# Stick-breaking attention without the "less one" step, with more of the FFN in the hand-made order

## The chip, the cores and the metric

One Trainium2 chip, of which the kernel uses one core. The metric is device time of one execution, in microseconds (us). Engines are named as the profile names them: PE (TensorE matmul), PEld (TensorE weight load), DVE (VectorE), ACT (ScalarE), POOL (GpSimd), SP (SyncE, which here mostly issues DMAs).

## The reference, cut to what matters

One decoder layer on x of 1024 tokens x 1024 features, float32:

```
h = rms_norm(x);  q, k, v, glu_a, glu_b = split(h @ w_in)      # 512 columns each
q, k normed per head of 64
beta[t,s] = sigmoid(q_t . k_s / 8),  s < t
A[t,s]    = beta[t,s] * prod_{s<j<t} (1 - beta[t,j])
attn_t    = sum_{s<t} A[t,s] v_s                               # 8 heads
c = swish(layer_norm(causal_conv31(glu_a * sigmoid(glu_b))))
x = x + concat(attn, c) @ w_out
h = rms_norm(x);  gate, val = split(h @ w_up)                  # 2816 columns each
x = x + (silu(causal_conv3(gate)) * val) @ w_down
```

With S[t,s] the product of (1 - beta[t,j]) over s <= j < t, and S = 1 from s = t on, a weight is the difference A[t,s] = S[t,s+1] - S[t,s]. So the sum over s can be made with S itself and the differences of neighbouring v, plus the last v of the range. The kernel before uses S - 1 in place of S, for which that last v drops out.

## The kernel before, in words

All products that need float32 accuracy are made of three matmuls in the fast type fp32r (`mm3`, L389 to L391): high times high, high times low, low times high. So each operand is first cast to its high part, on ACT mostly, and the low part is the difference, on DVE mostly. A matmul here has 128 x 128 weights and 512 columns; transposes are matmuls of 128 columns.

The kernel has three stretches. Two of them are laid out by a planner (`Plan`): every step is added with an engine or a choice of engines with a price in ns for each, with what it comes after and which buffers it takes, and `plan.run(ORDERS[0])` or `ORDERS[1]` walks through a written-out list of step numbers, picks the cheaper engine for the steps with a choice, and so fixes what stands in each engine's queue and in which order. Each engine then works through its queue in order and waits at the first instruction that isn't ready.

1. First plan. Idle matmuls at the start (`begin`, L485; five more at L499 that wait for the first input, L494). x is squared (ACT L530), its root taken (POOL L533, L534), scaled (DVE L548), transposed on PE to `hT` (L556) and split into `h_hi` (ACT L560) and `h_lo` (DVE L561). The weights of v are scaled by the norm's gain into `hi_v` (ACT L593) and `lo_v` (DVE L599); L715 makes v. v is differenced (POOL L656). q, k and the two glu halves follow, the convolution on DVE, ACT and POOL, then the attention. A head has four groups of 256 queries. For each row block of 128 queries PE makes z (L1304, L1305), ACT makes sigmoid(-z) into one of four buffers `nb` (L1312), DVE turns it into the running product from the right (the scan, L1326), POOL, or ACT, subtracts one in place ("less", L1331, L1333), PE transposes it, 128 x 128 at a time, into `wT` (L1353), which is split into a high part (ACT L1362, L1364, sometimes DVE) and a low part (DVE L1369, L1374) and multiplied with the differenced v into the bank `po` (L1381). The blocks on the diagonal have a half that isn't written; it is cleared to zero once. Two groups, one of each half of `po`, end in a copy (ACT L1409) and a sum (DVE L1412) into `attn`. Between these, PE does the convolution's half of w_out as filler (`op`); its weights are split by ACT L1438 and DVE L1439, those of the attention's half (`hio`, `loo`) by ACT L1526 and DVE L1531.
2. Second plan. The attention's half of w_out (`opa`; its operand `m` is split by ACT L1599, L1607 and DVE or POOL L1605, L1608), the second norm (DVE L1622, L1640, ACT L1632), transposes to `h2T` (PE L1648) and their split (`b`, `bT`: ACT L1660, DVE or POOL L1661; copies and sums of them at L1673, L1693 to L1698). FFN up works on quarters of its operands with seven products in place of eight, named 11, 12, 22, S1 to S4 after the sums that go in; sums of the weights are made at L1733 to L1739 and L1795, their splits at L385, L386, L1784 and L1788. The first two products of the first column block (f = 0) lie in this plan.
3. The rest, without a planner: FFN up for the remaining products of 22 column blocks, its gate (L1834, L1836), and FFN down (`dn`, L1987).

DMAs are issued on SP in the order in which the plan puts them.

## Time and profile before

| | us |
|---|---|
| median of 3 runs (lowest to highest) | 1103.04 (1102.15 to 1103.22) |
| the profiled execution | 1100.73 |
| its span in the trace | 1099.0 |
| PE busy | 1085.8 |
| DVE, ACT, POOL busy | 875.4, 606.6, 609.8 |
| granted TensorE clock | 1.00 in all stretches |

Lines of a timeline read: start, duration, engine, line of the code, operation, out<-in, shape, xcount of equal neighbours, and in brackets how long the engine (or the instruction) waited before it and on whom. Lines of the table by stretch read: from:to, length, then busy time and count of PE, PEld, DVE, ACT, POOL, the granted clock, the share of the DMA engines and GB/s. A busy PE overlaps with the next instruction, so a matmul that lasts 0.39 us in a timeline starts about 0.23 us behind the one before it. Lines of the grouped views give a count, the busy time and the mean in ns, or min/median/max in ns.

### The profile page before, as it was taken

What the parts mean: (1) busy time and instruction counts of PE and PEld (TensorE: products, weight loads), DVE (VectorE), ACT (ScalarE), POOL (GpSimd) and SP (SyncE); (2) the same over time, 40 slices, a digit from 0 to 9 for tenths busy, and PEclk for the clock granted to TensorE, in tenths of its full rate; (3) what the DMA queues carried; (4) which work ended last, traced back from release to release, by engine and by line L of the source; (5) the groups of instructions that cost most, each with busy time, mean ns of one, the idle gap of its engine ahead of it and who ended that gap; (6) DMA issues with size and microseconds to landing.
All of it is one profiled execution on the core that took longest, in us unless ns stands there. A gap on an engine that the chain in (4) does not pass through costs nothing.

```text
span 1099.0 us, 14945 instructions
## 1 busy us (share of the span) xinstructions
PE 1085.8 (99%) x5252; PEld 904.1 (82%) x5252; DVE 875.4 (80%) x1178; ACT 606.6 (55%) x1113; POOL 609.8 (55%) x540
## 2 busy tenths in 40 slices
PE   8999999999999999999999999999999999999998
PEld 5888888889888878778888888888888888888887
DVE  6498898689998996899977777677867578697885
ACT  7345467878877665644433333333433388676660
POOL 3377988786654544784333223313322399887760
PEclk9999999999999999999999999999999999999999
DMA  8121210444643324523322312222222572413403
GB/s 272 39 58 52 83 39 19 116 154 143 203 125 97 106 94 161 187 58 116 96 96 67 104 59 96 77 96 77 77 97 67 183 287 78 153 31 124 153 7 147
DMA packets 110249, 117.99 MB, mean 107 GB/s; under 512 B 21114, under 2 KB 89953, under 8 KB 110175
## 3 DMA queue, kind: packets, MB, share of 16 engines
q1 hardware_dynamic: 110158, 117.05, 32.5%
q8 instruction: 41, 0.67, 0.3%
q14 instruction: 34, 0.27, 0.1%
q10 hardware_dynamic: 16, 0.00, 0.0%
HBM read 82.43 MB, written 28.31 MB: 101 GB/s over the span
## 4 chain that ended last, share of the span: by engine, by line
PE 92%; DVE 3%; ACT 1%; DMA 1%; issue 1%; POOL 1%; SPq 0%; DVEq 0%; ACTq 0%
PE dn L1987 19%; PE u_S L391 7%; PE u_S L390 7%; PE u_S L389 7%; PE u L391 5%; PE u L390 5%; PE u L389 5%; PE po L1381 3%; PE qk L389 3%; PE qk L391 3%; PE qk L390 3%; PE wT L1353 2%; PE z L1304 1%; PE glu_b L390 1%; PE op L389 1%; PE glu_b L391 1%
## 5 line engine op out<-in xcount | busy, mean ns | idle before, releaser
L1987 PE MATMUL dn<-wd,wd 128*128 128x512 f32 x768 | 181.4, 389 | 0.0
L1987 PEld LDWEIGHTS dn<-wd,wd 128*128 128x128 f32 x768 | 144.1, 188 | 29.9
L1990 DVE TENSOR_TENSOR c<-dn,c 128x512 f32<-128x512 f32 x120 | 81.4, 685 | 27.6 <-PE dn L1987 27.0
L391 PE MATMUL u_S<-bT,aS 128*128 128x512 f32 x264 | 102.7, 389 | 0.1
L390 PE MATMUL u_S<-bT,aS 128*128 128x512 f32 x264 | 102.5, 389 | 0.0
L389 PE MATMUL u_S<-bT,aS 128*128 128x512 f32 x264 | 102.5, 389 | 0.0
L385 ACT CAST aS<-rawu 128x512 fp32r<-128x512 f32 x63 | 39.0, 621 | 95.2 <-PE u_S L391 68.9
L1892 ACT CAST wd<-rawd 128x512 fp32r<-128x512 f32 x128 | 72.6, 618 | 31.8 <-DMA rawd<-act_d 8.0
L1326 DVE TENSOR_TENSOR_SCAN nb<-nb,one 128x128 f32<-128x128 f32 (+7 forms) x64 | 85.1, 1341 | 1.5 <-ACT nb L1312 1.4
L1733 POOL TENSOR_TENSOR s<-rawu 128x512 f32<-128x512 f32 x21 | 29.6, 1414 | 101.8 <-DMA rawu<-in_w_up_dram 101.8
L1891 ACT COPY whole<-rawd 128x512 f32<-128x512 f32 x110 | 63.4, 585 | 26.0 <-DVE wd L1893 12.9
L1739 POOL TENSOR_TENSOR rawu<-rawu 128x512 f32<-128x512 f32 x21 | 29.5, 1408 | 81.1 <-DVE a L386 81.1
L1893 DVE TENSOR_TENSOR wd<-whole,wd 128x512 fp32r<-128x512 f32 x90 | 59.9, 684 | 12.6 <-ACT wd L1892 6.8
L1331 POOL TENSOR_SCALAR nb<-nb 128x512 f32<-128x512 f32 (+7 forms) x57 | 39.8, 705 | 50.3 <-DVE nb L1326 38.0
L1836 DVE SCALAR_TENSOR_TENSOR y<-gv,cols_a,y 128x1023 f32<-128x1023 f32 (+1 forms) x44 | 59.9, 1361 | 8.9 <-ACT y L1834 8.9
L385 ACT CAST a<-rawu 128x512 fp32r<-128x512 f32 x63 | 38.9, 621 | 48.7 <-PE u_S L391 33.8
L389 PE MATMUL u<-b,a 128*128 128x512 f32 x168 | 65.5, 390 | 0.0
L391 PE MATMUL u<-b,a 128*128 128x512 f32 x168 | 65.4, 389 | 0.0
L390 PE MATMUL u<-b,a 128*128 128x512 f32 x168 | 65.3, 389 | 0.0
L386 DVE TENSOR_TENSOR a<-rawu,a 128x512 fp32r<-128x512 f32 x63 | 50.9, 809 | 13.3 <-ACT a L385 13.3
L1735 POOL TENSOR_TENSOR rawu<-s,rawu 128x512 f32<-128x512 f32 x21 | 32.0, 1527 | 48.6 <-DVE a L386 47.8
L391 PEld LDWEIGHTS u_S<-bT,aS 128*128 128x128 f32 x264 | 49.5, 188 | 10.7 <-DVE aS L386 0.5
(359 smaller groups left out, 3274.5 us busy)
## 6 DMA issues: line engine op xcount, KB each, us to landing
rawu<-in_w_up_dram SPq DMA_DIRECT2D x44, 512.0 KB
act_d<-y SPq DMA_DIRECT2D x22, 512.0 KB
rawd<-act_d SPq DMA_DIRECT2D x22, 512.0 KB
rawd<-in_w_down_dram SPq DMA_DIRECT2D x22, 512.0 KB
raw_qk<-in_w_in_dram SPq DMA_DIRECT2D x16, 256.0 KB
rawo<-in_w_out_dram SPq DMA_DIRECT2D x8, 512.0 KB
m<-conv_d SPq DMA_DIRECT2D x16, 256.0 KB
xt<-in_x_dram SPq DMA_DIRECT2D x8, 512.0 KB
```

The source lines that it names most:

```text
L385: nc.scalar.copy(hi, src)
L386: lo_engine.tensor_tensor(lo, src, f32(hi), op=ALU.subtract)
L389: nc.tensor.matmul(ps, a_hi, b_hi, start=first, stop=False)
L390: nc.tensor.matmul(ps, a_hi, b_lo, start=False, stop=False)
L391: nc.tensor.matmul(ps, a_lo, b_hi, start=False, stop=last)
L1326: nc.vector.tensor_tensor_scan(rev, rev, ones_of[0][:, :w], 0.0, op0=ALU.mult, op1=ALU.max)
L1836: nc.vector.scalar_tensor_tensor(y[:, j:], g[:, :S - j], par("fw", (KF - 1 - j) * NF + f), y[:, j:], op0=ALU.mult, op1=ALU.add)
L1891: nc.scalar.copy(whole, src)
L1892: nc.scalar.copy(t[:, 0], src)
L1893: lo_engine.tensor_tensor(t[:, 1], whole, f32(t[:, 0]), op=ALU.subtract)
L1987: nc.tensor.matmul(ps, a[:, tok], b, start=first and m == 0, stop=last and m == 2, skip_group_check=True)
L1990: nc.vector.tensor_tensor(sums[c][s], ps, sums[c][s], op=ALU.add)
```

## The change

The diff's parts, then its core:

- The scanned products go to the transposes as they are. The 64 "less" steps are gone. Unwritten halves of the diagonal blocks hold ones in the high part instead of zeros. For each group of 256 keys the last v joins the sum: `take_ends` issues four tiny DMAs for each half of the heads (8 in all), PE transposes them (4 transposes), DVE copies them to `v_ends`; the differencing of v waits for these DMAs as well. `summed` becomes two instructions of 256 columns that add `po`, the last v and the copy.
- 9 idle matmuls at the start instead of 7.
- More steps have a choice of engines: scaling x (ACT too), the casts to `h_hi` (DVE too), the high part of v's weights (DVE too), scaling q and k (POOL and ACT too), the low parts of both halves of w_out (POOL too). Prices in the planner are changed, some by much (the load time of DMAs from 3250 to 3500 ns).
- The second plan knows of the end of the first (two empty steps), and it also holds the remaining five products of f = 0 with their sums, and the first two products of f = 1 with their weights' load and split.
- Both lists of step numbers are new. In counts: DVE's instructions go from 1180 to 1203, ACT's from 1099 to 1030, POOL's from 545 to 506, SP's from 304 to 312, PE's from 5267 to 5275.

```diff
 ORDERS = ...
-1 35 37 14 36 49 2 0 39 41 50 38 40 45 42 3 5 8 51 43 6 16 46 55 11 44 52 119 53 122 56 130 128 15 4 121 28 125 54 25
+1 35 14 37 49 0 36 39 50 38 40 2 41 45 42 43 3 44 46 119 122 5 8 6 51 47 52 48 16 124 26 55 53 54 121 56 7 9 57 128
...
-        for n in range(7):
+        for n in range(9):
...
-            c = add("DVE", 690, lambda i=i, cols=cols: nc.vector.tensor_scalar(xt[:, cols], xt[:, cols], d["rs"], None, op0=ALU.mult),
+            c = add({"DVE": 560, "ACT": 650}, lambda eng, i=i, cols=cols: (
...
-            f = add("ACT", 600, lambda i=i, where=where: nc.scalar.copy(h_hi[t // 4][where], d["pt", i]), T(at_ + 1), [m])
+            f = add({"ACT": 600, "DVE": 690}, lambda eng, i=i, where=where: (nc.scalar.copy if eng == "ACT" else nc.vector.tensor_copy)(
+                h_hi[t // 4][where], d["pt", i]), T(at_ + 1), [m])
...
-            a = add("ACT", 1190, high, T(at_ - LEAD_W), [x, begun_at], d["rooms"])
-            b = add({"DVE2": 1400, "POOL": 3700}, low, T(at_ - LEAD_W + 0.5), [a])
+            a = add({"ACT": 1330, "DVE": 1120}, high, T(at_ - LEAD_W), [x, begun_at], d["rooms"])
+            b = add({"DVE2": 1480, "POOL": 3700}, low, T(at_ - LEAD_W + 0.5), [a])
...
+        def take_ends():
+            d["ends"] = squares(room, f"ends{blk}")[:4, :256]
+            for n in range(4):
+                nc.sync.dma_start(d["ends"][n:n + 1, :], qkv["v", blk][P - 1:P, 2 * n + 1, :])
+
+        def turn_ends():
+            d["turned"] = bank(s, [P, 2, 4], f"ends{blk}")
+            for c in range(2):
+                nc.tensor.transpose(d["turned"][:, c, :], d["ends"][:, c * P:(c + 1) * P], ident[:4, :4])
+
+        y = add("SP", 2000, take_ends, key, after, [room])
...
-            subs.append(add({"POOL": 2414}, sub, key, [x]))
+            subs.append(add({"POOL": 2414}, sub, key, [x, y]))
...
-                nc.scalar.copy(diagonal(blk, name)[:, :P], zero_b)
+                nc.scalar.activation(diagonal(blk, name)[:, :P], zero_b, AF.Identity, bias=plus_one if name == "thd" else 0.0)
...
-                def less(eng, d=d, o=o):
-                    nb = d["nb"][:, o:S]
-                    if eng == "POOL":
-                        nc.gpsimd.tensor_scalar(nb, nb, 1.0, -1.0, op0=ALU.mult, op1=ALU.add)
-                    else:
-                        nc.scalar.activation(nb, nb, AF.Identity, bias=minus_one)
-
                 a = add("DVE", 130 + 2.1 * w, scan, i - AHEAD_SCAN + 0.3 * u, ones)
-                b = add({"POOL": 192 + 0.84 * w, "ACT": 296 + 0.84 * w}, less, i - AHEAD_SCAN + 0.3 * u, [a])
-                ws.append((b, d, nbt, o))
+                ws.append((a, d, nbt, o))
...
-                def summed(dst=dst, pd=pd, pa=pa):
-                    nc.vector.tensor_tensor(dst(), pd["po"].rearrange("p a t -> p (a t)")[pa, :], dst(), op=ALU.add)
+                def summed(dst=dst, pd=pd, pa=pa, h=h, half=half):
+                    for a in range(2):
+                        to = dst()[:, a * 256:(a + 1) * 256]
+                        end = 4 * (h // 2) + 2 * half + a
+                        nc.vector.scalar_tensor_tensor(to, pd["po"][pa, a, :], v_ends[pa, end:end + 1], to, op0=ALU.add, op1=ALU.add)
...
-        b = add("DVE2", 1215, lambda: nc.vector.tensor_tensor(w_attn[k][1], d["raw"], f32(w_attn[k][0]), op=ALU.subtract), key, [a])
+        b = add({"DVE2": 1215, "POOL": 2450}, lambda eng: (nc.vector if eng == "DVE" else nc.gpsimd).tensor_tensor(w_attn[k][1], d["raw"], f32(w_attn[k][0]), op=ALU.subtract), key, [a])
...
+    attention_ends = add("PE", 2000, lambda: None, -9.0)
+    last_sums = add("DVE", 790, lambda: None, -8.0, [add("ACT", 690, lambda: None, -8.5, [attention_ends])])
...
-        for e, a, b in ((e11, "11", "11"), (e12, "12", "21")):
-            add("PE", 2730, lambda a=a, b=b: begun.update({a: product_up(0, A, a, b)}), BEGIN_AT, e + block_done[b], [plan.token("o")])
+        _, x1, x2 = first_two(0, ready, BEGIN_AT, [])
+        key = BEGIN_AT + 1
...
+        first_two(1, next_ready, key, attn_read)
+        q, tq = product(0, "S4", "22", key + 0.2, e_s4)
+        s2p, t2 = product(0, "S2", "T2", key + 0.4, e_s2)
...
+        s3p, t3 = product(0, "S3", "T3", key + 0.7, e_s3)
...
+        s1p, t1 = product(0, "S1", "T1", key + 1.0, e_s1)
...
+        p22, t22 = product(0, "22", "T4", key + 1.3, e22)
```

What the new lists do to the engines' queues is shown at three places. The first is PE's queue at the start, from the first transposes of h on; before:

```order
L556 MATMUL hT_0_223<-ident_r,x_k_138 128x128 x4
L556 MATMUL hT_1_245<-ident_r,x_k_138 128x128 x4
L556 MATMUL hT_0_255<-ident_r,x_k_138 128x128 x4
L715 MATMUL v_260<-hi_v_228,h_hi_175 128x512 x2
L556 MATMUL hT_1_266<-ident_r,x_k_138 128x128 x4
L715 MATMUL v_260<-hi_v_240,h_lo_176 128x512
```

and in the changed kernel:

```order
L556 MATMUL hT_0_225<-ident_r,x_k_138 128x128 x4
L556 MATMUL hT_1_236<-ident_r,x_k_138 128x128 x4
L739 MATMUL v_241<-hi_v_231,h_hi_175 128x512 x2
L556 MATMUL hT_0_258<-ident_r,x_k_138 128x128 x4
L739 MATMUL v_241<-hi_v_231,h_lo_176 128x512 x2
L556 MATMUL hT_1_271<-ident_r,x_k_138 128x128 x4
```

The first two products of v now stand ahead of the transposes of the second row of tiles of x. With them, ACT casts the first `h_hi` ahead of everything else and scales the second tile of x, and DVE scales the first two pieces of v's weights.

The second place is DVE's queue at the end of the attention (head 7, its last group): the scan of the last row block, casts and low parts of wT, low parts of w_out (`loo`), the sum; before:

```order
L1531 TENSOR_TENSOR loo2_4296<-rawo_3078,hio2_4295 128x1024
L1326 SCALAR_TENSOR_TENSOR nb0_7_2432<-nb0_7_2432,one_2173 128x1024
L1374 TENSOR_TENSOR tl_2354<-wT7_2_0_4319,rest_2182 128x512
L1364 CAST rest_2182<-wT7_2_1_4331 128x512
L1374 TENSOR_TENSOR tl_2354<-wT7_2_1_4331,rest_2182 128x512
L1369 TENSOR_TENSOR diagonal_1_3285<-wT7_2_2_4337,diagonal_1_3285 128x384
L1374 TENSOR_TENSOR tl_2354<-wT7_3_0_4359,rest_2182 128x512
L1531 TENSOR_TENSOR loo1_4348<-rawo_3078,hio1_4347 128x1024
L1369 TENSOR_TENSOR diagonal_1_3285<-wT7_3_3_4364,diagonal_1_3285 128x384
L1374 TENSOR_TENSOR tl_2354<-wT7_3_1_4382,rest_2182 128x512
L1374 TENSOR_TENSOR tl_2354<-wT7_3_2_4391,rest_2182 128x512
L1531 TENSOR_TENSOR loo3_4404<-rawo_3078,hio3_4403 128x1024
```

and in the changed kernel:

```order
L1355 SCALAR_TENSOR_TENSOR nb0_2_2246<-nb0_2_2246,one_2085 128x1024
L1395 TENSOR_TENSOR tl_2352<-wT7_2_0_4257,rest_2156 128x512
L1390 TENSOR_TENSOR diagonal_1_3336<-wT7_2_2_4266,diagonal_1_3336 128x384
L1395 TENSOR_TENSOR tl_2352<-wT7_2_1_4273,rest_2156 128x512
L1395 TENSOR_TENSOR tl_2352<-wT7_3_0_4279,rest_2156 128x512
L1385 CAST rest_2156<-wT7_3_1_4299 128x512
L1395 TENSOR_TENSOR tl_2352<-wT7_3_1_4299,rest_2156 128x512
L1390 TENSOR_TENSOR diagonal_1_3336<-wT7_3_3_4305,diagonal_1_3336 128x384
L1395 TENSOR_TENSOR tl_2352<-wT7_3_2_4321,rest_2156 128x512
L1556 TENSOR_TENSOR loo3_4345<-rawo_3323,hio3_4344 128x1024
L1436 SCALAR_TENSOR_TENSOR attn_110<-po7_2_4256,v_ends_103,attn_110 64x256 x2
```

Two low parts of w_out have left DVE here; they stand in POOL's queue, as does a third one earlier. Behind the sum the casts of `m` on ACT stand in the same order as before.

The third place is PE's queue in the second plan where FFN up begins; before, from the last opa product of token tile 7 on:

```order
L391 MATMUL opa7_1_4909<-hio2_4295,m7_4800 128x512
L1648 MATMUL h2T3_0_4931<-ident_r_118,h2_3_4899 128x128 x4
L1648 MATMUL h2T3_1_4938<-ident_r_118,h2_3_4899 128x128 x4
L389 MATMUL u0_11_4957<-b11_4435,a_first_4893 128x512
L390 MATMUL u0_11_4957<-b11_4435,a_first_4893 128x512
```

and in the changed kernel:

```order
L390 MATMUL opa7_1_4825<-hio2_4214,m7_4737 128x512
L1678 MATMUL h2T3_0_4849<-ident_r_118,h2_3_4804 128x128 x4
L1678 MATMUL h2T3_1_4855<-ident_r_118,h2_3_4804 128x128 x4
L1678 MATMUL h2T6_1_4861<-ident_r_118,h2_6_4734 128x128 x4
L388 MATMUL u0_11_4889<-b11_4368,a_first_4819 128x512
L389 MATMUL u0_11_4889<-b11_4368,a_first_4819 128x512
```

Four transposes of token tile 6 now stand between those of tile 3 and the first product. Behind u0_11 and u0_12 come the transposes of tile 7, then u1_12 and u1_11 (before: u1_11, u1_12), and then S3, S2, S1, 22, S4 of f = 0 (before: S2, S3, S1, S4, 22). On POOL this stretch now also holds more of the sums and low parts of the weights of f = 1.

More of the change, by code (lines that the diff above doesn't have):

```diff
@@ L651, in differences @@
         x.moves = [Plan.FEW, Plan.MIXED, Plan.FEW] * 2
+        room, s = plan.token("squares"), plan.token("s")
+        def take_ends():
[7 more added lines that the diff above has]
+        y = add("SP", 2000, take_ends, key, after, [room])
+        y.moves = [Plan.FEW] * 4
+        m = add("PE", 230, turn_ends, key, [y], [s])
+        kept_ends = add("DVE", 100, lambda: nc.vector.tensor_copy(v_ends[:, 8 * blk:8 * blk + 8].rearrange("p (c t) -> p c t", c=2), d["turned"]), key, [m])
+        room.users += [y, m]
+        s.users += [kept_ends]
+        done["ends", blk] = kept_ends
         subs = []
@@ L1140, in queries_keys @@
         c = add("POOL", 1925, lambda: rstd(d["rs"], d["sq"], 1.0 / DH), key(0.5), [b])
[L1141 removed]
+        e = add({"DVE": 750, "ACT": 2750}, scale, key(0.5), [c])
         room.users += [b]
@@ new lines, in first_operands, with gate_values @@
+        ready = {"11": e11, "12": e12, "22": e22, "S1": e_s1, "S2": e_s2, "S3": e_s3, "S4": e_s4}
+        made, gates = {}, []
+        def gate_values(f):
+            if not gv:
+                both = mixp.tile([P, 3, S], F32, tag="attn", name="gv")
+                gv.extend(both[:, k, :] for k in range(3))
+            if f and len(gv) < 4:
+                gv.append(mixp.tile([P, S], F32, tag="attn_2", name="gv_3"))
+            g, v = gv[f % 2], gv[2 + f % 2]
+            return {"g0": g[:, :HS], "g1": g[:, HS:], "v0": v[:, :HS], "v1": v[:, HS:]}
@@ new lines, in product, with plus, emit @@
+        def product(f, a, b, key, needs):
+            t = plan.token("o" if f == 0 and a in ("11", "12") else "z")
+            made[f, a] = add("PE", 2730, lambda: banks_of.update({(f, a): product_up(f, A if f == 0 else A_next, a, b, t.name)}),
+                             key, needs + block_done[b], [t])
+            return made[f, a], t
+        def plus(f, dst, a, src, key, m, after):
+            def emit():
+                p = gate_values(f)
+                nc.vector.tensor_tensor(p[dst], banks_of[f, a], p[src], op=ALU.add)
+            return add("DVE", 690, emit, key, [m] + after)
@@ new lines, in first_two @@
+        def first_two(f, needs, key, after):
+            p1, t1 = product(f, "11", "11", key, needs["11"])
+            p2, t2 = product(f, "12", "21", key, needs["12"])
+            x1 = add("ACT", 600, lambda: nc.scalar.copy(gate_values(f)["v0"], banks_of[f, "11"]), key + 0.1, [p1] + after + ([p2] if f == 0 else []))
+            x2 = plus(f, "g0", "12", "v0", key + 0.1, p2, [x1])
+            t1.users += [x1]
+            t2.users += [x2]
+            return p1, x1, x2
+        _, x1, x2 = first_two(0, ready, BEGIN_AT, [])
@@ L1818, in product @@
         def product(a, b):
-            return begun.pop(a) if f == 0 and a in begun else product_up(f, A, a, b)
+            return product_up(f, A, a, b)
         tt = nc.vector.tensor_tensor
@@ L1840, in up @@
         nc.sync.dma_start(act_d[f], y)
-    gv = mixp.tile([P, 3, S], F32, tag="attn", name="gv")
-    gv = [gv[:, k, :] for k in range(3)] + [mixp.tile([P, S], F32, tag="attn_2", name="gv_3")]
     for f in range(NF):
```

128 lines of the change are left out of this document (91 added, 37 removed), and 161 rows, old and new, of the table ORDERS.

## The prediction

> **What bounds the kernel now.** I read the page first, then the table by stretch, then PE's waits, then the timelines of the places where PE stands still. The page's first part, and of the table by stretch those rows that matter:
>
> ```profile
> PE 1085.8 (99%) x5252; PEld 904.1 (82%) x5252; DVE 875.4 (80%) x1178; ACT 606.6 (55%) x1113; POOL 609.8 (55%) x540
> ```
>
> ```profile
> 0.00:12.00 12.00, 8.68 (x35) 3.96 (x36) 4.91 (x16) 8.10 (x16) 2.61 (x11) 1.00 0.85 285
> ...
> 220.00:402.00 182.00, 180.67 (x1180) 159.92 (x1179) 167.45 (x204) 138.84 (x287) 113.40 (x123) 1.00 0.42 129
> 402.00:411.00 9.00, 6.92 (x52) 5.99 (x50) 8.26 (x12) 6.28 (x11) 2.43 (x3) 1.00 0.49 165
> ...
> 455.00:476.00 21.00, 18.57 (x88) 14.48 (x88) 20.69 (x27) 15.58 (x29) 17.93 (x16) 1.00 0.49 151
> ...
> 500.00:1099.00 599.00, 595.29 (x2627) 492.58 (x2625) 457.85 (x615) 283.65 (x461) 280.39 (x208) 1.00 0.30 104
> ```
>
> PE is the bound: 1085.8 of 1099.0 us, and the granted clock is 1.00 everywhere. PE's idle time is 1099.0 - 1085.8 = 13.2 us. Of that 3.32 us lie in the first 12, 1.33 in the attention (220 to 402), 2.08 in its tail (402 to 411), 2.43 at the start of FFN up (455 to 476). After 500 a matmul comes every 595.29 / 2627 = 0.227 us and the only idle 3.71 us are the last sums and stores, which the change leaves alone. So nothing can be gained beyond 13.2 - 3.7 = 9.5 us, 0.9%, and the removal of 39.8 us of POOL's work by itself gains nothing: POOL isn't the bound. What counts is which of PE's few waits go, and which come. Three rows of the list of waits; the longest of the others stand in the timelines below:
>
> ```profile
> PE hT L556 <- DVE x_k L548: 1.2, 2, 0.7
> ...
> PE kT L1226 <- DVE rest L1267: 0.6, 1, 0.6
> ...
> PE z L1304 <- ACT nb L1312: 0.5, 2, 0.3
> ```
>
> **The change part by part.**
>
> *Start.* The timeline of the first 12 us:
>
> ```profile
> 3.48 0.88 PE L485 MATMUL idle<-zero_b 128*128 128x512 bf16 x2
> ...
> 5.04 1.58 PE L499 MATMUL idle<-go,zero_b 128*128 128x512 bf16 x5 [0.68 <-DVE go L494]
> ...
> 6.63 0.88 DVE L548 TENSOR_SCALAR x_k<-x_k,rs 128x512 f32<-128x512 f32 x2 [0.90 <-POOL rs L534]
> ...
> 7.17 1.10 PE L556 MATMUL hT<-ident_r,x_k 128*128 128x128 f32 x8 [0.56 <-DVE x_k L548]
> ...
> 7.98 1.34 ACT L593 ACTIVATE hi_v<-raw_v,gain 128x512 fp32r<-128x512 f32 x2 [0.56 <-DMA raw_v<-in_w_in_dram]
> ...
> 9.22 0.56 ACT L560 CAST h_hi<-hT 128x512 fp32r<-128x512 f32 x1
> ...
> 9.84 0.73 PE L715 MATMUL v<-hi_v,h_hi 128*128 128x512 f32 x2 [0.22 <-ACT h_hi L560]
> ...
> 11.13 0.50 PE L715 MATMUL v<-hi_v,h_lo 128*128 128x512 f32 x1
> ```
>
> Two more idle matmuls are 0.88 us. They fill the 0.68 us ahead of 5.04; the five behind then end 0.20 us later, near 6.82, still ahead of 7.17: nothing. (Without that cover they cost 0.88.) The first product of v waits for a cast that ACT makes only after 1.34 us of weights. Now the cast comes first: the transposes of its half are over at 7.17 + 0.55, the cast at about 8.3. The weights' high part moves to DVE, from the DMA's landing at 7.98. Its two instructions are not in the trace; two scalings of 512 columns on DVE took 0.88 (at 6.63), the same work on ACT 1.34, and I take the first, as it is the same engine: 8.9. So v starts 0.94 us earlier. Of that, four transposes that now come behind it take back 4 x 1.10 / 8 = 0.55; and the stall of 11.13 - 9.84 - 2 x 0.227 - 0.55 = 0.29 goes, since two products of v now wait there. Together 0.94 - 0.55 + 0.29 = 0.68. If DVE takes 1.34, 0.2. The second tile of x is now scaled on ACT, ahead of PE by little, and one low part goes to POOL, which could cost some tenths. Taken: -0.6, between -0.9 and +0.3.
>
> *The "less" steps, sums and casts.* DVE is the second busiest engine in the attention: idle 182 - 167.45 = 14.55 us to 402, and 0.74 in the tail. Rows by form of DVE from 220 to 411:
>
> ```profile
> L1267 DVE SCALAR_TENSOR_TENSOR rest<-qT,qgain,keys 128x512 fp32r<-128x512 f32 x16 | 11.8, 736 | 0.9 <-ACT keys L1264 0.9
> L1412 DVE TENSOR_TENSOR attn<-po,attn 64x512 f32<-64x512 f32 x12 | 8.2, 684 | 1.2 <-ACT attn L1409 0.8
> ...
> L1439 DVE TENSOR_TENSOR w_hl<-rawo,w_hh 128x1024 fp32r<-128x1024 f32 x4 | 5.7, 1444 | 0.0
> ...
> L950 DVE TENSOR_TENSOR conv_lo<-conv_out,conv_hi 128x512 fp32r<-128x512 f32 x4 | 3.2, 794 | 0.4 <-ACT conv_hi L939 0.4
> L1133 DVE TENSOR_TENSOR qk<-qk,rs_qk 128x256 f32<-128x256 f32 x8 | 3.0, 412 | 0.0
> ...
> L1364 DVE CAST rest<-wT 128x512 fp32r<-128x512 f32 x2 | 1.4, 680 | 0.0
> ```
>
> A sum of 256 columns is not in the trace. Half of L1412's 0.684 is 0.34, the row of 256 columns has 0.412, and a scalar_tensor_tensor lasts 0.05 more than a plain cast of its width (0.736 against 0.680); the upper bound is the whole 0.684. I take 0.412 + 0.05 = 0.46, nearest to the row of the same width. With p for it, 16 sums of two cost 16 x (2p - 0.684) = 32p - 10.9 more. Casts that move from ACT: 6 of wT and 2 of keys, 8 x 0.68 = 5.4. What leaves DVE: three `loo` (1.22 each, below), two w_hl, two conv_lo: 3.7 + 2.9 + 1.6 = 8.2. DVE's work grows by 32p - 13.7: +1.0 at 0.46, -2.8 at 0.34, +8.2 at 0.684. Against 15.3 us of idle time +1.0 is nothing by itself. PE's waits there (kT, z and smaller ones) sum up to 1.3; with the order made anew I let 0.3 of it go. Taken: -0.3, between -1.3 and the rival below. The 39.8 us of POOL and the 5 of ACT are worth their latency only, and PE has filler (`op`) ahead of nearly all of it; if that cover were gone a group would wait for its "less", 1.04 us at most.
>
> *Tail of the attention,* where no filler is left:
>
> ```profile
> 400.11 2.29 DVE L1326 TENSOR_TENSOR_SCAN nb<-nb,one 128x1024 f32<-128x1024 f32 x1
> ...
> 402.49 1.04 POOL L1331 TENSOR_SCALAR nb<-nb 128x1024 f32<-128x1024 f32 x1 [0.33 <-DVE nb L1326]
> ...
> 405.50 1.22 DVE L1531 TENSOR_TENSOR loo<-rawo,hio 128x1024 fp32r<-128x1024 f32 x1
> ...
> 407.10 1.40 DVE L1374 TENSOR_TENSOR tl<-wT,rest 128x512 fp32r<-128x512 f32 x2
> ...
> 407.83 0.39 PE L1381 MATMUL po<-tl,rest 128*128 128x256 f32 x1 [0.41 <-DVE tl L1374]
> ...
> 409.68 1.80 SPq L1594 DMA_DIRECT2D x<-x_part  x3
> 409.69 0.58 ACT L1409 COPY attn<-po 64x512 f32<-64x512 f32 x1 [0.97 <-PE po L1381]
> ...
> 410.49 1.05 ACT L1607 CAST m<-attn 128x384 fp32r<-128x384 f32 x2
> ...
> 411.05 0.50 PE L389 MATMUL opa<-hio,m 128*128 128x512 f32 x1 [1.40 <-ACT m L1607]
> ```
>
> From the scan's end at 402.40 the last group needs its "less", then its low parts, one after the other on DVE, with a `loo` of 1.22 us between; the last low part ends at 408.50. Now the "less" and that `loo` are gone from the chain (the `loo` is on POOL, which has nothing else to do then). By DVE's queue that is 1.22 us; but PE's own idle time ahead of 409.7 is only 2.08 - 1.35 = 0.73, and some tenths of late starts with it. I take 0.9 and the bounds 0 and 1.2. The wait of 1.40 for the cast of `m` stays: ACT's copy, a small cast and the cast follow each other as before, and the sum isn't ahead of that cast. Late next is this copy. Taken: -0.9.
>
> *Start of FFN up.*
>
> ```profile
> 461.56 1.04 PE L1648 MATMUL h2T<-ident_r,h 128*128 128x128 f32 x8
> 463.40 0.50 PE L389 MATMUL u<-b,a_first 128*128 128x512 f32 x1 [0.81 <-ACT b L1660]
> 464.49 0.47 PE L390 MATMUL u<-b,a_first 128*128 128x512 f32 x1 [0.59 <-DVE b L1661]
> ...
> 469.59 0.39 PE L391 MATMUL u<-b,a_first 128*128 128x512 f32 x1
> 470.68 1.29 PE L1648 MATMUL h2T<-ident_r,h 128*128 128x128 f32 x8 [0.71 <-ACT gv L1825]
> ```
>
> By starts, u comes 463.40 - 461.56 - 1.04 = 0.80 late, its second matmul 464.49 - 463.40 - 0.227 = 0.86, the transposes of tile 7 470.68 - 469.59 - 0.227 = 0.86: 2.5 us. Four transposes of tile 6 now lie in the first gap (0.5), and on DVE the copies of tile 3 no longer stand ahead of the low parts of `b`; I count 1.2 of the first two gaps as gone, and half of the third, whose cause is a scaling of h queued on DVE behind low parts of weights that were stretched beside POOL: 0.4. Taken: -1.6, between -2.5 and +2, which the second rival explains.
>
> *Added for good.* Four transposes: at 1.10 / 8 each 0.55 at most, 0.4 taken. Eight DMA issues on SP at 1.80 / 3 = 0.6 each stand ahead of loads of weights, and the differencing on POOL waits for them; the projections of q, k and glu lie between and hide this. If not, one issue's delay is 0.6. The clears with ones, the empty steps and the new prices cost nothing.
>
> Sum: -0.6 - 0.3 - 0.9 - 1.6 + 0.4 = -3.0. Span 1096.0; the profiled execution 1100.73 has 1.73 around its span, so 1097.7; the median of before lies 2.31 above the profiled run, so about 1100.0.
>
> **The rivals.** Below, 0.2% is 2.2 us, about what a measurement of this kernel can tell from no change (its three runs lie 1.07 apart).
>
> *All waits but the fixed ones go* (the empty steps let the plan see the tail): up to 9.5; at half to nearly full 1094 to 1098. Against it: each gap's last releaser is a queue on DVE or ACT which stays nearly as full. 0.10.
>
> *POOL becomes late in FFN up.* POOL is busy 17.93 of 21 us from 455 to 476, and from there on it now makes more of the sums and low parts of f = 1 that PE needs soon. What one costs:
>
> ```profile
> L1487 POOL TENSOR_TENSOR xt<-prod,xt x16: 1272/1292/2100, 290.5 to 403.5; 128x512 f32<-128x512 f32 x16
> ```
>
> ```profile
> L386 DVE TENSOR_TENSOR a<-rawu,a x6: 680/1774/1778, 466.9 to 499.2; 128x512 fp32r<-128x512 f32 x6
> ```
>
> About 15 of them at 1.3 are 20 us, at the slower 1.7 that lies between median and longest 26, and DVE's low parts go from 0.68 to 1.77 beside them. A chain that is 2 us later than planned makes a product of f = 0 or f = 1 wait as long, which takes back the 1.6: -1.4, about 1101.6. 0.18.
>
> *The change does little where it counts*: the removed step was hidden, the gaps keep their size behind new causes: -0.5 to +0.5, 1103. 0.14.
>
> *Slower: DVE becomes the bound of the attention.* If DVE's extra work finds none of the idle time, since that is latency behind ACT in a queue that runs in order, PE pays 32p - 13.7. Slower by 2.2 needs 2.2 plus the gains elsewhere (0.6 + 1.6 - 0.4 = 1.8), so 4.0, which is p = 0.55 us for a sum of 256 columns. At 0.684 it is 8.2 - 1.8 = +6.4, 1109; between, 1106 to 1109. For it: DVE is busy 92%. Against it: the row of 256 columns has 0.412. 0.14.
>
> *Scans stretched by POOL.* POOL gets three `loo`, two w_hl and two conv_lo, that is 12 pieces of 512 columns with two inputs in SBUF, beside scans:
>
> ```profile
> L1326 DVE TENSOR_TENSOR_SCAN nb<-nb,one 128x1024 f32<-128x1024 f32 x8 | 18.2, 2280 | 0.7 <-ACT nb L1312 0.6
> ```
>
> If each stretched a scan as L386 is stretched (1.77 - 0.68 = 1.09), 13 us would come on DVE, of which more than 4 on PE makes it slower: 1105 to 1112. The trace speaks against it: the eight longest scans average 2.280 us, and the one at 400.11 lasted 2.29 beside POOL's work. 0.02. The Trainium skill ("GPSIMD Engine Reference", 1. Specifications) says that POOL shares its SBUF interfaces with VectorE, with contention for DVE instructions with two SBUF inputs; a scan is one. By that rule the time is this rival's; by the rows, the rule holds for L386 and not for the scan, and the sum stays.
>
> **How the numbers follow.** Forecast as worked out, 2.2 to 5 us faster: 0.42. Faster in all 0.42 + 0.10 = 0.52; same 0.18 + 0.14 = 0.32; slower 0.14 + 0.02 = 0.16. The likeliest is 1100.0, its own range 1098 to 1100.8. From 1095.5 to 1104.5 leaves out the slower cases and the end of the best.
>
> **What would show it.** Right: v's first product near 8.9; the copy of the last `po` 0.9 earlier against the start of that group; the gaps at u0_11 under 0.6 together; sums of 0.41 to 0.5; scans as long as before. Wrong: a table by stretch in which PE's idle time from 220 to 402 is above 3 us, a sum of 0.55 and more, or waits on POOL's low parts between 476 and 500.

## The result, and the profile after

| | before | after |
|---|---|---|
| median (lowest to highest), us, 20 runs each | 1102.84 (1101.14 to 1103.58) | 1104.68 (1102.70 to 1107.18) |
| ratio, 95% interval | | 1.0021 [1.0014, 1.0027] |
| profiled execution, its span, us | 1100.73, 1099.0 | 1106.51, 1104.6 |

The change made the kernel slower, by 0.21% in the ratio and by 1.84 us between the medians (the ratios given here differ a little from the quotients of the medians). Forecast were some 3 us the other way, 1100.0.

An execution's mean granted clock takes few values, nearly always 1.000, 0.998, 0.997 or 0.995, and the time goes with it: 27 executions of before that stand beside one set of experiments have medians of 1101.45 (3 at 1.000), 1102.6 (16 at 0.998) and 1104.0 (8 at 0.997). After has 1102.7 (1 at 1.000), 1103.9 (8), 1105.2 (7) and 1106.55 (4 at 0.995). So at the same clock it is some 1.2 us slower, and it also falls behind in clock more often, which makes the other 0.6. The two profiles overstate this second part: the one of before has the clock at 1.000, the one of after at 0.995, and their spans differ by 5.6 us where the medians differ by 1.84.

The first line of after's page, and rows of its table by stretch, cut where PE stood still or ran slow:

```profile
PE 1091.2 (99%) x5258; PEld 908.6 (82%) x5258; DVE 882.3 (80%) x1201; ACT 586.5 (53%) x1044; POOL 591.0 (53%) x501
```

```profile
0.00:12.00 12.00, 9.06 (x35) 4.08 (x35) 4.94 (x15) 6.86 (x14) 5.05 (x14) 1.00 0.80 270
...
15.00:19.00 4.00, 4.00 (x12) 3.10 (x11) 4.00 (x8) 2.87 (x5) 1.81 (x4) 0.57 1.03 407
...
220.00:402.00 182.00, 181.38 (x1181) 160.04 (x1180) 167.10 (x225) 125.34 (x249) 91.92 (x84) 1.00 0.44 134
...
414.00:419.00 5.00, 3.97 (x11) 3.11 (x12) 1.93 (x5) 1.37 (x4) 0.46 (x1) 0.66 0.66 262
...
455.00:476.00 21.00, 20.68 (x105) 17.14 (x104) 20.40 (x27) 14.57 (x29) 19.46 (x20) 1.00 0.60 189
476.00:479.00 3.00, 1.31 (x5) 0.48 (x3) 3.00 (x2) 3.00 (x6) 2.92 (x3) 1.00 0.01 3
479.00:483.00 4.00, 3.71 (x9) 2.95 (x10) 4.00 (x8) 1.75 (x4) 2.66 (x3) 0.57 0.14 43
```

PE is idle for 13.4 us (1104.6 - 1091.2) where it was 13.2: the sum of the waits hardly moved. PE is *busy* 5.4 us longer. A column that the argument had passed over says why: the granted clock is 0.57 to 0.66 in three stretches, behind a wait each time. There a matmul of 512 columns takes 0.427 us from start to start, instead of 0.227.

Worked out from the starts of all matmuls in the two traces (an interval longer by 0.15 to 0.21 us is put down to the clock, more to a wait, the rest to PE's work and small delays):

| us, after less before, to the last matmul's start | work at full clock and small | waits | slow clock |
|---|---|---|---|
| start to the first product of opa | 1.9 | 0.1 | 2.0 |
| first opa product to the first of u | -0.4 | -1.4 | 1.2 |
| first of u to FFN down | 0.1 | 0.7 | 1.6 |

Of the 1.9 us of work in the first row, 0.85 are the two added idle matmuls, which fill time at the start in which PE would wait, and 0.4 the four added transposes. Without the slow clock the three rows come to +2.0, -1.8 and +0.8.

PE's list of waits names the new ones in its first two rows; the third was there before:

```profile
PE v L739 <- DVE hi_v L598: 3.7, 2, 1.9
PE u L390 <- DVE a L1903: 2.0, 1, 2.0
PE opa L388 <- ACT m L1637: 1.4, 1, 1.4
```

*Start.* The timeline of after:

```profile
8.91 0.88 DVE L598 TENSOR_SCALAR hi_v<-raw_v,gain 128x512 fp32r<-128x512 f32 x2 [1.94 <-DMA raw_v<-in_w_in_dram]
...
9.54 0.80 PE L739 MATMUL v<-hi_v,h_hi 128*128 128x512 f32 x2 [1.82 <-DVE hi_v L598]
...
10.37 3.44 DVE L598 TENSOR_SCALAR hi_v<-raw_v,gain 128x512 fp32r<-128x512 f32 x2
...
11.12 2.41 POOL L608 TENSOR_TENSOR lo_v<-raw_v,hi_v 128x1024 fp32r<-128x1024 f32 x1
```

```profile
13.87 0.96 PE L739 MATMUL v<-hi_v,h_hi 128*128 128x512 f32 x3 [1.86 <-DVE hi_v L598]
```

The first pair of scalings takes 0.88, as forecast. The second pair takes 3.44: POOL makes the low part that the change let it have until 13.53, and the scalings end behind it, at 13.81. PE stands 1.86 us, and the clock is 0.57 from 15 to 19. The same wait stands in the profiles of the three other kernels that keep this start, 2.12 or 2.13 us from matmul start to matmul start (here 2.14), without a slow clock behind it.

*Tail of the attention.* The same places as before, from the last scan on:

```profile
404.56 2.29 DVE L1355 TENSOR_TENSOR_SCAN nb<-nb,one 128x1024 f32<-128x1024 f32 x1
...
412.53 0.38 PE L1402 MATMUL po<-tl,rest 128*128 128x256 f32 x1 [0.34 <-DVE tl L1395]
...
413.66 0.58 ACT L1430 COPY attn<-po 64x512 f32<-64x512 f32 x1 [0.96 <-PE po L1402]
...
415.03 0.80 PE L388 MATMUL opa<-hio,m 128*128 128x512 f32 x1 [1.41 <-ACT m L1637]
415.62 0.63 PE L389 MATMUL opa<-loo,m 128*128 128x512 f32 x1
```

From the scan's start to the copy are 9.10 us, before 9.58 (400.11 to 409.69): 0.5 shorter, not 0.9. But two filler matmuls (`op`) fewer lie in that stretch, 5 where 7 were, which is 0.45 us of PE's work done earlier. From the scan's start to the first opa product PE is idle 2.03 us, before 2.14, so next to nothing of the 0.5 is a gain. Behind the 1.41 us wait the clock has fallen (0.427 from 415.62 to the next).

*FFN up.*

```profile
472.37 1.79 DVE L1691 TENSOR_TENSOR bT<-t,bT 128x512 fp32r<-128x512 f32 x1
...
473.58 1.73 POOL L1832 TENSOR_TENSOR rawu<-rawu,rawu 128x512 f32<-128x512 f32 x1
...
474.09 1.77 DVE L1691 TENSOR_TENSOR bT<-raws,bT 128x512 fp32r<-128x512 f32 x1
...
475.40 1.62 POOL L1832 TENSOR_TENSOR rawu<-s,rawu 128x512 f32<-128x512 f32 x1
...
475.79 1.77 DVE L1825 TENSOR_TENSOR a<-rawu,a 128x512 fp32r<-128x512 f32 x1
...
475.90 0.62 ACT L1899 CAST a<-rawu 128x512 fp32r<-128x512 f32 x1 [3.04 <-DVE bT L1691]
...
477.49 1.75 DVE L1903 TENSOR_TENSOR a<-rawu,a 128x512 fp32r<-128x512 f32 x1
...
479.29 0.56 PE L390 MATMUL u<-b,a 128*128 128x512 f32 x1 [1.98 <-DVE a L1903]
479.65 0.63 PE L388 MATMUL u<-b,a 128*128 128x512 f32 x1
```

DVE's low parts take 1.75 to 1.79 here, four in a row, beside the sums of weights that the longer second plan puts on POOL. ACT's cast of the weights for f = 1 waits 3.04 for a buffer, its low part comes last, and PE stands 1.98 us at L390, with a slow clock behind it.

### The profile page after: what moved, and what is told of

It reads as the page before. It is cut to its first block, busy times and chain, and to the rows that moved or that the text cites. A ratio compares the mean times of both kernels' runs of the same rounds, so it can differ in the third digit from the quotient of the medians.

```text
span 1104.6 us, 14843 instructions
## 1 busy us (share of the span) xinstructions
PE 1091.2 (99%) x5258; PEld 908.6 (82%) x5258; DVE 882.3 (80%) x1201; ACT 586.5 (53%) x1044; POOL 591.0 (53%) x501
## 4 chain that ended last, share of the span: by engine, by line
PE 96%; DVE 2%; ACT 1%; DMA 1%; issue 0%; SPq 0%; POOL 0%; DVEq 0%; POOLq 0%
PE dn L2099 19%; PE u_S L388 7%; PE u_S L389 7%; PE u_S L390 7%; PE u L390 5%; PE u L388 5%; PE u L389 5%; PE po L1402 3%; PE wT L1374 3%; PE qk L388 3%; PE qk L390 3%; PE qk L389 3%; PE z L1333 2%; PE z L1334 1%; PE opa L388 1%; PE opa L390 1%
## 5 line engine op out<-in xcount | busy, mean ns | idle before, releaser
L390 PE MATMUL u_S<-bT,aS 128*128 128x512 f32 x264 | 102.6, 389 | 0.0
L1355 DVE TENSOR_TENSOR_SCAN nb<-nb,one 128x384 f32<-128x384 f32 (+7 forms) x64 | 85.0, 1341 | 1.1 <-ACT nb L1341 0.9
L390 PE MATMUL u<-b,a 128*128 128x512 f32 x168 | 66.0, 393 | 2.0 <-DVE a L1903 2.0
L389 PEld LDWEIGHTS u_S<-bT,aS 128*128 128x128 f32 x264 | 49.6, 188 | 10.3
L388 PEld LDWEIGHTS u_S<-bT,aS 128*128 128x128 f32 x264 | 49.6, 188 | 10.3
L390 PEld LDWEIGHTS u_S<-bT,aS 128*128 128x128 f32 x264 | 49.6, 188 | 10.3
```

The source lines that it names most:

```text
L388: nc.tensor.matmul(ps, a_hi, b_hi, start=first, stop=False)
L389: nc.tensor.matmul(ps, a_hi, b_lo, start=False, stop=False)
L390: nc.tensor.matmul(ps, a_lo, b_hi, start=False, stop=last)
L1355: nc.vector.tensor_tensor_scan(rev, rev, ones_of[0][:, :w], 0.0, op0=ALU.mult, op1=ALU.max)
```

## The experiments

All times are medians; each ratio is against the kernel before, measured beside it on the same chip, with its 95% interval.

### Which half of the change

**The first plan alone.** Edit: everything of the change up to the second plan; from there on the kernel before, with its list.

```diff
-ORDERS = (before's first list, before's second list)
+ORDERS = (after's first list, before's second list)
```

> The changed first plan (start, projections, attention) with the second plan and all behind it as before. Theory: the two waits of 2.0 us at the start stay, with a slow clock behind them in many executions, and FFN up has before's waits of 2.5 us in place of the changed one's 2.2 plus slow clock: 0.5 to 1.5 us below the changed kernel, so about 1 us above before. Rival (all of the loss lies in the second plan): at or below before.

Measured: 1105.79 against 1102.60, 1.0024 [1.0015, 1.0034]. The loss lies in the first plan, and it is larger than the theory had: 3.2 us above before, where about 1 was expected, and no better than the whole change.

**The second plan alone.** Edit: the other way round.

```diff
-ORDERS = (before's first list, before's second list)
+ORDERS = (before's first list, after's second list)
```

> The first plan as before, with the changed second plan. Theory: the wait of 2.2 us in front of the second product of f = 1 and the slow clock behind it stay, against before's three waits of 2.5 us without: 0 to 1.5 us above before. Rival (all of the loss lies in the first plan): 1 us or more below before.

Measured: 1102.26, 0.9998 [0.9990, 1.0007]: neither gain nor loss, between the theory and the rival. Its profiled execution has the stop near 476 too, and a clock of 0.66 behind it.

### What in the first plan: the less step, the sum, the last values

**All three in the old order.** Edit: the kernel before, with the less steps empty, the sum in two and the last values fetched, turned and added, at fixed places in before's list.

```diff
-                b = add({"POOL": 192 + 0.84 * w, "ACT": 296 + 0.84 * w}, less, ...)
+                b = add("POOL", 0, lambda: None, ...)
...
-                    nc.vector.tensor_tensor(dst(), ... pd["po"] ..., dst(), op=ALU.add)
+                    for a in range(2):
+                        nc.vector.scalar_tensor_tensor(to, pd["po"][pa, a, :], v_ends[pa, end:end + 1], to, ...)
```

> The kernel before with the first part of the change alone: no less steps, ones in the diagonal's unwritten halves, the last v of each 256 keys added in two instructions of 256 columns; order and choices of engines as before (one cast of keys and two scalings change engine by themselves). Theory (the loss comes from the new order: three long waits of PE, and a TensorE clock that is halved for about 3.3 us behind each in many executions): 0 to 1 us faster than before, since only the tail's chain gets shorter; PE idle from 220 to 402 stays near 1.3 us. Rival (the sums make DVE the bound of the attention): 1 to 3 us slower, with PE idle above 3 us from 220 to 402.

Measured: 1105.67 (9 runs), 1.0029 [1.0019, 1.0039]. The buffer of the last values is written by another step before they are read, so other numbers are added; the work is the same. The theory fell: it is 3.1 us slower, not up to 1 faster. The rival has the size but not the sign it named: PE's idle time from 220 to 402 is 182 - 180.39 = 1.61, not above 3. Its timeline near the end of the attention:

```profile
401.62 1.29 POOL L1513 TENSOR_TENSOR xt<-prod,xt 128x512 f32<-128x512 f32 x1 [9.87 <-ACT prod L1510]
401.66 2.32 DVE L1557 TENSOR_TENSOR loo<-rawo,hio 128x1024 fp32r<-128x1024 f32 x1
...
404.01 2.29 DVE L1355 TENSOR_TENSOR_SCAN nb<-nb,one 128x1024 f32<-128x1024 f32 x1
```

The low part of w_out takes 2.32 where it took 1.23 before; it starts 0.04 us behind a sum on POOL, and the last scan queues behind it.

**The same, with that low part moved.** Edit: a buffer of its own for the last values, and that `loo` behind a later low part in the list.

```diff
-            d["ends"] = attn_row(3)[:4, 256:512]
+            d["ends"] = cp.tile([P, 512], F32, tag="squares0", ...)[:4, :256]
```

> The kernel before with the first part of the change alone, as in less_only, with the last values taken through another buffer, and one low part of w_out (loo2) moved on DVE from ahead of the last scan to behind two low parts of wT. In less_only it came 0.04 us behind an addition on POOL and took 2.32 us instead of 1.23, since sums that take 0.2 longer had moved it there. Theory (this meeting made the removal slower): the attention, from the first product with v to the last, takes 0.8 to 1.6 us less than less_only's 174.67, and the time comes to 0 to 1.5 us above before. Rival (16 longer sums in DVE's queue are the cost): it stays above 174 and the time 2.5 to 3.5 above before.

Measured: 1105.82 (5 runs), 1.0036 [1.0023, 1.0049]. The meeting is gone and the time isn't: other waits came, 1.07 us at the third opa product, 0.87 in the last group, 0.80 ahead of the last values' transposes. That the one meeting was the cause has fallen. The time is the rival's, 3.1 above before, but the rival's cause doesn't hold either: the longer sums by themselves cost 0.1 (below).

**The less step alone.**

```diff
-                b = add({"POOL": 192 + 0.84 * w, "ACT": 296 + 0.84 * w}, less, ...)
+                b = add("POOL", 0, lambda: None, ...)
```

> The kernel before without the 64 less steps and nothing in their place: the sum stays one instruction of 512 columns, no last values are fetched, turned or added, so the output lacks the last value of each group and the halves that aren't written stay zero. Order and engines otherwise as before. Theory (DVE's and POOL's steps come earlier and meet others that they missed before, above all a low part of w_out and a sum on POOL near 401.6): as long as the kernel with the sums and last values, 1104 to 1105.5, with longer DVE instructions beside POOL. Rival (sums, transposes and DMAs of the last values cost what that kernel lost): 1102.0 to 1102.6, the attention shorter by some tenths.

Measured: 1101.26 against 1102.77, 0.9990 [0.9981, 0.9999]. The theory fell: leaving the steps out is a gain of 1.5 us, more than the rival had. It isn't quite the step alone: with the steps priced at nothing the planner also moves two casts of `keys` from ACT to POOL and a scaling of q or k from ACT to DVE, here and in the two kernels above. From the first po product to the last are 172.16 us, before 172.89; the tail in it, however, has its old length to the hundredth:

```profile
400.31 2.29 DVE L1326 TENSOR_TENSOR_SCAN nb<-nb,one 128x1024 f32<-128x1024 f32 x1
402.51 0.67 DVE L1367 TENSOR_TENSOR tl<-wT,rest 128x512 fp32r<-128x512 f32 x1
...
409.88 0.58 ACT L1402 COPY attn<-po 64x512 f32<-64x512 f32 x1 [0.96 <-PE po L1374]
```

From scan to copy 9.57 us, before 9.58. DVE goes from the scan at once to the low parts of the row blocks before it, here as in the kernel before, whose row is

```profile
402.32 0.67 DVE L1374 TENSOR_TENSOR tl<-wT,rest 128x512 fp32r<-128x512 f32 x1
```

(402.51 - 400.31 = 2.20, before 402.32 - 400.11 = 2.21). So the last block's "less" of 1.04 us lay beside DVE's work.

**The sum in two alone.** Edit: two instructions of 256 columns that add a zero; the less steps stay.

```diff
-                    nc.vector.tensor_tensor(dst(), ... pd["po"] ..., dst(), op=ALU.add)
+                    for a in range(2):
+                        nc.vector.scalar_tensor_tensor(to, pd["po"][pa, a, :], 0.0, to, ...)
```

> The kernel before, in which only the sum of 512 columns at the end of two groups becomes two of 256 columns that also add a zero; nothing else is changed, the less steps stay. Theory (DVE has room for it, 16 times 0.2 us, and PE sees little): 1102.6 to 1102.9. Rival (the longer sums are what the attention lost when the less steps went): 1.8 more in the attention, 1104.5, ratio 1.0017.

Measured: 1102.86, 1.0003 [0.9994, 1.0012]. The theory held.

```profile
L1414 DVE SCALAR_TENSOR_TENSOR attn<-po,attn x24: 389/419/428, 242.0 to 411.4; 64x256 f32<-64x256 f32 x24
```

**The last values alone.** Edit: fetched, turned and copied, but added nowhere; the less steps and the single sum stay.

```diff
+            for n in range(4):
+                nc.sync.dma_start(d["ends"][n:n + 1, :], qkv["v", blk][P - 1:P, 2 * n + 1, :])
...
+                nc.tensor.transpose(d["turned"][:, c, :], d["ends"][:, c * P:(c + 1) * P], ident[:4, :4])
```

> The kernel before with only the fetching of the last values added: eight small DMAs on SP, four transposes on PE, two copies on DVE, and the differencing of v that waits for the DMAs. Nothing adds these values; the less steps and the single sum stay. So far, against the kernel before: less steps gone alone 1.5 faster, sums in two alone 0.1 slower, all together 2.8 to 3 slower. Theory (fetching the last values is what costs: a late transpose stops PE, the DMAs push loads back): 1105 to 1106, with PE waits at the transposes and behind them. Rival (each part is cheap, and only together do the steps on DVE fall beside POOL's): 1102.8 to 1103.5, 0.4 of it the transposes.

Measured: 1104.01 against 1102.68, 1.0013 [1.0004, 1.0022]. It lies between the two theories. The trace accounts for about 1.0 us of it: four transposes, and 0.61 us from start to start ahead of the second pair, which waits for DVE:

```profile
263.63 0.40 PE L391 MATMUL qk<-hi_qk,h_lo 128*128 128x512 f32 x1
264.47 0.28 PE L662 MATMUL ends<-ident_r,ends 4*128 4x4 f32 x2 [0.44 <-DVE tl L1404]
```

In the changed kernel's own trace this wait is missing: its second pair starts 0.33 us behind the matmul before it, 0.1 more than that matmul takes.

The three parts alone make -1.5 + 0.1 + 1.3 = -0.1 us, each with an interval of about 1 us to either side. Together, in the old order, they make +3. That their costs don't add up is more than these intervals allow; that meetings on DVE carry the other 3 us is likely but not shown, and which of them do is not settled.

### What the waits cost

**Idle matmuls in the tail's wait, before and after.** Edit: six bf16 matmuls of zeros ahead of the first opa product, about 1.4 us, which is the length of the wait.

```diff
                 d["ps", nn] = pso.tile([P, 512], F32, tag="bank", name=f"opa{t}_{nn}")
+                if t == 0 and nn == ...:
+                    for _ in range(6):
+                        nc.tensor.matmul(d["ps", nn]..., zero_b, ..., start=True, stop=True)
```

> The kernel before with six idle matmuls (bf16, into the bank that the first opa product overwrites) in front of the first opa product, where PE waits 1.6 us for the cast of m. Theory (a wait of this length lets the granted clock fall to half in some executions, and filling it prevents that): the times lose their upper part, median 1.0 to 1.5 us below before, no execution with a clock under 1.00. Rival (the fall of the clock has nothing to do with waits): median within 0.4 us of before, spread as before.

> The changed kernel with six idle matmuls in front of the first opa product, as they were tried in the kernel before. Theory: 0.8 to 1.3 us below the changed kernel, mean granted clock of its executions up by about 0.001. Rival (slow clock there has another cause): within 0.4 us of it.

Measured: before with them 1101.61, 0.9991 [0.9982, 0.9999]; after with them 1103.85, 1.0011 [1.0003, 1.0020], where after alone had 1.0021 [1.0014, 1.0027]. The first is a gain, if only just; the second lies as forecast, but the intervals overlap. Nothing waits less, and PE does more. That no execution would have a clock under 1.00 was too much: 6 of the 11 of before with them have 0.997 to 0.999. And at the same clock these are still 0.6 to 0.7 us shorter than before's (1100.93 against 1101.64 at 1.000, 1102.01 against 1102.61 at 0.998), so not all of the 1.0 us is the clock. After's stretch behind the tail now reads

```profile
414.00:419.00 5.00, 4.95 (x22) 3.77 (x21) 2.17 (x4) 0.04 (x1) 0.00 (x0) 1.00 0.39 152
```

with a clock of 1.00. Of the profiled executions of all kernels that keep that wait (1.68 us from the start of the last po product to that of the first opa product), 5 of 11 have a slow stretch behind it (1.2 to 1.6 us of excess); of the three with idle matmuls none has. So few executions decide little by themselves; the medians of the runs point the same way.

**The start's low part on DVE.** Edit: after with every engine choice fixed, the first `lo_v` on DVE in place of POOL, and two entries at the start of the list exchanged.

```diff
-"ESSDPSDD...
+"ESSDDSDD...
```

> The changed kernel with every choice of engine held, but the low part of the first weights of v on DVE in place of POOL (its three instructions there took 3.9 us beside DVE's second scaling, which took 3.44 for two). Theory (a DVE instruction that comes second waits until POOL's instruction with two inputs is over): that scaling takes 0.9 to 1.4 again, PE's wait of 2.0 us at 11.8 falls under 0.8, fewer executions have a slow clock; 0.8 to 1.6 us below the changed kernel, 0.3 to 1.2 above before. Rival (the wait comes from the load of the weights): the wait stays within 0.4 us, and so does the time.

Measured: 1104.63, 1.0014 [1.0005, 1.0023]. The stretched scaling is gone (0.89 again) and so is its wait. A new one came later in its place:

```profile
25.64 2.40 POOL L652 TENSOR_TENSOR lo_glu_b<-raw_glu_b,hi_glu_b 128x1024 fp32r<-128x1024 f32 x1 [0.43 <-ACT hi_glu_b L641]
26.32 2.79 DVE L636 TENSOR_TENSOR raw_glu_a<-raw_glu_a,gain 128x1024 f32<-128x1024 f32 x1 [1.85 <-DMA raw_glu_a<-in_w_in_dram]
...
30.59 0.63 PE L581 MATMUL hT<-ident_r,x_q 128*128 128x128 f32 x4 [2.56 <-DVE h_lo L587]
```

The scaling of 1.22 us takes 2.79, since it starts while POOL works. So the time stayed that of after, and the 0.8 to 1.6 us that the theory expected did not come. The edit moved the meeting; its own worth can't be read from this run. The new wait is the longest of all, and the clock stays at 1.00 behind it; the paragraph on the clock below says why.

**The sums of weights for f = 0 on DVE.** Edit: after with every engine choice fixed, the totals s1 and s3 (L1839, L1840) on DVE.

```diff
-"APAPADPPPAPADAPP...
+"APAPADDDPAPADAPP...
```

> The changed kernel with every choice of engine held, but the first two sums of the weights of f = 0 (s1, s3) on DVE in place of POOL, where they run beside DVE's low parts of bT. Theory (DVE's low parts take 1.77 instead of 0.68 beside them, and so hold the buffer that the first operand of f = 1 waits for): those low parts take 0.7 again, PE's wait of 2.2 us in the first product with it falls under 1.0 and its slow clock goes; 1 to 2 us below the changed kernel. Rival (two more sums of 0.68 on DVE cost as much as they free): within 0.5 us of it.

Measured: 1103.62, 1.0003 [0.9994, 1.0012]: 1.1 us less than after by the medians, and the intervals of the two ratios don't overlap. The low parts of bT take 0.68 again, and the 1.98 us at L390 is gone; two waits of 0.67 and 0.63 came at the next products, and the clock stays at 1.00:

```profile
474.00:478.00 4.00, 3.33 (x15) 2.48 (x14) 3.99 (x6) 3.05 (x7) 3.92 (x4) 1.00 0.43 124
478.00:483.00 5.00, 4.37 (x19) 3.18 (x18) 3.00 (x3) 1.52 (x3) 5.00 (x4) 1.00 0.02 6
```

Here the profiles are clear: a slow stretch in all four kernels with these totals on POOL (each with its wait of some 2 us), in none of the two with them on DVE and none of the eight with before's second plan.

### The parts that are worth it, together

**Before's first plan, after's second plan with those totals on DVE, six idle matmuls in the tail.**

> The kernel before's first plan, the changed kernel's second plan and rest, in that plan the two totals s1 and s3 of f = 0 on DVE instead of POOL, and six idle matmuls ahead of the first opa product. Theory (the second plan's own gain is real and is taken back by POOL beside DVE, and the waits at the tail cost a fall of the clock in some executions): the second plan alone had 1102.3; the totals gave 1.06 and the idle matmuls 0.8 to 1.0 in other kernels, so 1100.4, a ratio of 0.998. Rival (both work through the same few falls of the clock, so they don't add up): 1101.3, a ratio of 0.9988. Rival (the gains belong to the kernels they were seen in): 1102.3, 1.000.

Measured: 1100.30 (1099.71 to 1101.62) against 1102.77, 0.9980 [0.9971, 0.9989], as the theory had it. So the gains add up, as far as the interval tells: its upper end just takes in the 0.9988 of the rival in which they don't. Seven of its 11 executions have a clock of 1.000, the other four 0.998. The tail and FFN up of the profiled one:

```profile
410.15 1.47 PE L1633 MATMUL opa<-zero_b 128*128 128x512 bf16 x6
411.71 0.50 PE L398 MATMUL opa<-hio,m 128*128 128x512 f32 x1
```

```profile
PE u_S L399 <- DVE bT L1678: 0.7, 1, 0.7
PE u_S L400 <- POOL aS L1812: 0.6, 1, 0.6
...
PE u L399 <- DVE b L1678: 0.3, 1, 0.3
```

The opa products follow the last po as they did before (411.71 - 410.03 = 1.68): the idle matmuls save no wait. And the longest wait in FFN up is 0.7. About half of the 2.5 us is the clock: at 1.000 its median is 1100.11, where before has 1101.45.

## Why the prediction was wrong, point by point

**The step that failed first: what the first plan was to gain.** From the start to the first opa product the sum has -0.6 - 0.3 - 0.9 + 0.4 = -1.4 us. The traces have +2.0 there without any slow clock, and the first plan by itself makes the kernel 3.2 us slower. The largest part that has a name is the low part given to POOL at the start, put at "some tenths": PE waits 1.86 us for the scaling beside it. Of the gains taken for the attention and its tail next to nothing came. What else in the first plan costs stays open: the less step, the sum and the last values cost almost nothing one by one and 3 us together, in the old order.

**The step that failed second: a wait was counted at its own length, with the clock left out.** "The granted clock is 1.00 everywhere" was read off one execution without a fall of the clock, and in the runs shown above 3 of 27 are like it. The base itself was sound (1103.04, then 1102.84). But a fall costs 1.2 to 1.6 us, and counting 0.998 as one fall, 0.997 as two and 0.995 as three, after has 1.7 of them in an execution, before 1.2. That makes 0.6 us; the other 4 of the 4.7 us between forecast and result are there at equal clock. Idle time alone, the prediction's ceiling of 9.5 us, is not the whole ledger.

**Start, -0.6: wrong sign.** The first product was to come near 8.9; it came at 9.54, with the weights landing at 8.91 instead of 7.98, a time that varies between executions (with before's start the first product came at 9.84 to 11.18 in nine profiles, with after's at 8.69 to 9.79 in four). So the first product did come about a microsecond earlier, by the medians of these. What failed is "one low part goes to POOL, which could cost some tenths": the pair of scalings beside it took 3.44 in place of 0.88, PE waited 1.86, and in this execution the clock fell.

**Less, sums, casts, -0.3: the idle time went, the time didn't.** PE's idle time from 220 to 402 is 182 - 181.38 = 0.62, before 1.33. But from the first po product to the last, tail included, are 172.01 us, before 172.89, with five matmuls fewer in between (1126, before 1131), which are 0.9 us of work. So the stretch is as long as it was. The sum was taken at 0.46; it has 0.476, and the scans are as they were:

```profile
L1355 DVE TENSOR_TENSOR_SCAN nb<-nb,one 128x1024 f32<-128x1024 f32 x8 | 18.2, 2275 | 0.3 <-ACT nb L1341 0.2
...
L1436 DVE SCALAR_TENSOR_TENSOR attn<-po,v_ends,attn 64x256 f32<-64x256 f32 x24 | 10.5, 476 | 0.9 <-ACT attn L1430 0.8
```

So the rivals on the slower side named the wrong mechanisms: DVE did not become the bound there (167.10 busy from 220 to 402, before 167.45), and the scans weren't stretched, though one at 268.5 lay wholly beside POOL's instructions with two inputs (2.29). The kernel came out slower by other ones.

**Tail, -0.9: half by the chain, nothing for PE.** The "less" was read as a link of the chain because POOL's row stood behind the scan's. Without it alone the tail has its old length; that leaves the `loo` that left DVE, and the two filler matmuls that left PE, for the 0.5 us that came; neither was tried by itself. The trace of before had it: DVE began a low part at 402.32, ahead of the "less", and went on from there nearly without a gap.

**FFN up, -1.6: the gaps went as forecast, and the rest was the second rival.** Of the 2.5 us of gaps 0.59 are left. The wait at u0_11's second matmul is 467.53 - 466.71 - 0.227 = 0.59, and the first gap is gone:

```profile
465.44 1.47 PE L1678 MATMUL h2T<-ident_r,h 128*128 128x128 f32 x12
466.71 0.50 PE L388 MATMUL u<-b,a_first 128*128 128x512 f32 x1
467.53 0.47 PE L389 MATMUL u<-b,a_first 128*128 128x512 f32 x1 [0.32 <-DVE b L1691]
```

The rival "POOL becomes late", with the low parts at 1.77 beside it, took back 1.6 in words and 1.98 in the trace, between 476 and 500 as named, though PE waits for a low part on DVE there, not on POOL. Its price left out the clock, 1.6 us more in this execution. By itself the second plan measured -0.3 us, with an interval from -1.1 to +0.8.

**Added for good, +0.4: too low in the old order, not shown for the changed kernel.** Fetching the last values alone costs 1.3 us (0.4 to 2.4). The transposes were costed by their length; the wait in front of the second pair wasn't seen. In the changed kernel that pair hardly waits.

**A rule on the clock.** The rows first: each fall halves the clock for 3.41 us (6 to 8 matmuls at 0.427), at the same wait in some executions and not in others. The traces' record of the granted clock says when. Within a trace the falls start whole multiples of 3.413 us apart, wherever the waits are: in after at 15.37, 414.73 and 479.59, which is 117 and 19 steps. With that grid laid over the 14 traces from 4 us on, the 13 falls ahead of the last stores all start right behind a grid step in which PE was idle for 1.40 us or more. All six steps with more than 1.8 us idle were followed by one, 7 of the 19 with 1.40 to 1.72, and of the rest only one that lay in a fall already, which doubled it (6.83 us, at the start of before with idle matmuls). So what counts is how much idle time falls into one step. The tail's wait in before was cut, with 0.99 us idle in one step and 0.88 in the next, and the wait of 2.56 in `start_low_dve` was cut into 1.15 and 1.41: neither had a fall. What decides between 1.40 and 1.72 isn't shown.

The Trainium skill ("TensorE: Matmul & The Clock Gate", Part 1) has the clock decided by windows of 3413 ns that run freely, and names an idle window of about 3.4 us as what throttles. The windows agree with these traces; the amount of idle time doesn't, since about half a window was enough here.

## What to carry to other kernels

When the gap to close is a few microseconds, read the granted clock beside the waits: a wait that can cost a fall of the clock is worth more than its length, and idle matmuls in it can gain though the wait stays. Compare executions at the same clock, and not one profile with another. Before an operation is given to POOL because POOL is free, look at what DVE runs at that moment: scans apart, the one that starts second lasts until after the other has ended. And take a step out by itself before its gain is read off a chain: here the removal was worth 1.5 us, somewhere else than forecast, and with what replaced it the kernel lost 3.
